# Four projection tiles instead of three in the first k-loop, other warm-up products, and another order on VectorE around the first norm

## The chip, the cores and the metric

The kernel runs on one core of a Trainium2 chip. The metric is the device time of one execution in microseconds; less is better. Before the change three runs gave 1147.17, 1147.83 and 1149.77 us, median 1147.83 us.

## The reference

One transformer block in float32 on 1024 tokens of width 1024. Only its beginning matters here:

```python
mod = jax.nn.silu(c) @ w_ada[l] + b_ada[l]
sh1, sc1, g1, sh2, sc2, g2 = jnp.split(mod, N_MOD, axis=-1)
h = rms_norm(x, norm1_g[l]) * (1.0 + sc1[:, None]) + sh1[:, None]
z = h @ w_in[l]                     # 1024 x 1024 times 1024 x 2048
q = z[..., :A]; k = z[..., A:2*A]; v = z[..., 2*A:3*A]; u = z[..., 3*A:]
```

q, k and v go on to differential attention (q and k with a partial rotary), u to a pooling mixer; an output projection, a second norm, a routed mixture of 32 experts and a final norm follow.

## The kernel before

The kernel holds everything transposed: `xt[k]` is the k-th of eight blocks of 128 channels by 1024 tokens. Float32 products are made from halves: a value is split into a high part (ScalarE copies it to a shorter float, names in `h`) and a low part (VectorE subtracts the high part, names in `l`), and a product of two values is three matmuls, high by high, low by high, high by low. `split` (line 113) does this for every weight tile.

The stage of this case is the first projection, z = h w_in. Its 2048 output columns are 16 tiles of 128, in the order of `ORDER` (line 39): qr, kr, v0, q0, k0, u3, v1, u2 and so on. Tile m has its weights in `win`, split by `w_split(m)` into `wih` and `wil`; its sum stands in PSUM (`pz_...`), as 2 halves x 8 blocks k x 3 matmuls = 48 matmuls of 128x512.

Ahead of it (lines 308 to 339) the squares of `xt` are summed on ScalarE and VectorE (`ssq`), reduced on TensorE (`pss`), raised to the power -1/2 on GpSimd (`xr`), spread over all partitions by TensorE (`prs`, PSUM), and copied to SBUF by ScalarE (`rstd`). `warm` (line 317) issues matmuls whose result nobody reads, `pwarm`: 4 on each of four `xt` blocks as they land (`WARM`) and 8 between `pss` and `prs` (`WARM1`), each 128x128.

Then for each block k (lines 729 to 752): `norm1` multiplies `xt[k]` by `rstd` on VectorE, `norm1_high` makes `hh[k]` on ScalarE with the scale and shift of the conditioning (`gs`, `sh`), `norm1_rest` writes the unsplit value over `xt[k]` on ScalarE, `norm1_low` subtracts on VectorE (`hl[k]`). The scale and shift of block k are two sums over a 128x1024 slab of w_ada (`wa_sum`, VectorE, names in `wt`), finished by two small ScalarE instructions (`wa_add`). The loop runs two norms ahead and multiplies tiles 0 to 2 by block k as soon as that block is there; tile 0 and 1 are open in one PSUM pool (`pt`), tile 2 in another (`pw`). After the loop the code walks all 16 tiles: for m > 2 it multiplies tile m with all eight blocks at once, splits the weights of tile m + 1, evicts the finished tile, and lets VectorE do one or more of 32 further slab sums (`mod_row`, `MODS`).

The order on each engine is the order of the code: every instruction of TensorE, VectorE, ScalarE and GpSimd is kept in program order, and SyncE issues its DMAs in order. A tile framework adds the semaphore waits.

Of the kernel before, what the change touches and what calls it, by code (L numbers as in the profile page):

```python
# [13 lines left out]
AF = mybir.ActivationFunctionType  # L14
OP = mybir.AluOpType
# [3 lines left out]
P = 128  # L19
D = 1024  # L20
S = 1024
T = S // P
KD = D // P
# [15 lines left out]
ORDER = ["qr", "kr", "v0", "q0", "k0", "u3", "v1", "u2", "q1", "k1", "u1", "q2", "k2", "u0", "v2", "v3"]  # L39
# [13 lines left out]
STACK = (9, 10, 14)  # L53
FIRST = (16 - START) // 2
ML = 6
WARM = {3: 4, 4: 4, 5: 4, 6: 4}
WARM1 = 8
DOWN = 4
WQ = 5
YN = 2  # L60
# [7 lines left out]
def block_kernel(ctx: ExitStack, tc: tile.TileContext, A):  # L68
# [20 lines left out]
    def slab(name, shape=(1024,), dt=F32):  # L89
        n = int(np.prod(shape))  # L90
        t = big.tile([P, 1024], dt, name=name, tag="s")[:, :n]
        if len(shape) == 2:
            t = t.rearrange("p (a b) -> p a b", a=shape[0])
        elif len(shape) == 3:
            t = t.rearrange("p (a b c) -> p a b c", a=shape[0], b=shape[1])
        return t
# [4 lines left out]
    def dma(dst, src):  # L101
        tc.keep_in_program_order(nc.sync.dma_start(dst, src))  # L102
# [7 lines left out]
    def f(ap):  # L110
        return ap.bitcast(F32)

    def split(src, hi, lo, eng=None):
        act.activation(hi, src, AF.Copy)
        if eng is pool:
            pool_tt(lo, src, f(hi), OP.subtract)
        else:
            dve.tensor_tensor(lo, src, f(hi), op=OP.subtract)
# [31 lines left out]
    xt = []  # L150
# [93 lines left out]
    with tc.tile_pool(name="ps0", bufs=2, space=PSUM) as psum, tc.tile_pool(name="ps1", bufs=2, space=PSUM) as psum1, \  # L244
# [6 lines left out]
        def pt(name, shape=(1024,)):  # L251
            return shaped(psum.tile([P, 1024], F32, name=name, tag="p"), shape)

        def pw(name, shape):
            return shaped(psum1.tile([P, 512], F32, name=name, tag="w"), shape)
# [14 lines left out]
        def w_load(m):  # L270
            w = slab(f"win{m}", (KD, P))
            dma(w, A["w_in"][m])
            wsp[m] = w

        def w_split(m, eng=None):
            w = wsp[m]
            hi, lo = slab(f"wih{m}", (KD, P), F32R), slab(f"wil{m}", (KD, P), F32R)
            split(w, hi, lo, eng)
            wsp[m] = hi, lo
# [12 lines left out]
        def wa_sum(k, i):  # L292
            w = WA.pop((k, i))
            dve.scalar_tensor_tensor(w, w, 1.0, cB, op0=OP.mult, op1=OP.mult, accum_out=(gs, sh)[i][:, k:k + 1])

        def wa_add(k):
            for c, b, g in ((gs, bsc, n1g[:, k:k + 1]), (sh, bsh, 1.0)):
                c = c[:, k:k + 1]
                act.activation(c, c, AF.Identity, bias=b[:, k:k + 1], scale=g)
# [5 lines left out]
        w_load(1)  # L305
        wa_load(2)
        w_load(2)
        ssq = slab("ssq")
        for k in range(KD):
            sq = slab(f"sq{k}") if k else ssq  # L310
# [6 lines left out]
        def warm(x, n):  # L317

            for _ in range(n):
                pe.matmul(pwarm[:, 0:P], ident, x[:, 0:P], start=True, stop=True)  # L320

        for k, n in WARM.items():
            warm(xt[k], n)
# [7 lines left out]
        warm(xt[0], WARM1)  # L331
        prs = rows(pt("prs"), r8)
        rstd = slab("rstd")
        wa_sum(1, 0)
        w_split(0)
        wa_add(0)
        wa_sum(1, 1)
        act.activation(rstd, prs, AF.Copy)
        wa_add(1)

        hh, hl = [], []

        def norm1(k):
            dve.tensor_tensor(xt[k], xt[k], rstd, op=OP.mult)

        def norm1_high(k):
            hh.append(slab(f"hh{k}", dt=F32R))
# [17 lines left out]
        def project(m, h, ks, parts=(0, 1)):  # L365
            hi, lo = wsp[m]
            if m not in PZ:
                p = pt("pz_" + ORDER[m]) if m != 2 else None
                PZ[m] = [pw(f"pz_{ORDER[m]}_{i}", (512,)) if p is None else p[:, i * 512:(i + 1) * 512] for i in range(2)]
                PF[m] = p  # L370
            cs = slice(h * 512, (h + 1) * 512)
            for k in ks:
                if 0 in parts:
                    pe.matmul(PZ[m][h], hi[:, k], hh[k][:, cs], start=(k == 0), stop=False)
                    pe.matmul(PZ[m][h], lo[:, k], hh[k][:, cs], start=False, stop=False)
                if 1 in parts:
                    pe.matmul(PZ[m][h], hi[:, k], hl[k][:, cs], start=False, stop=(k == KD - 1))
# [58 lines left out]
        def plain(nm, pz):  # L436

            hi, lo = slab("th" + nm, dt=F32R), slab("tl" + nm, dt=F32R)
            if nm[0] == "q":
                act.activation(hi, pz, AF.Copy, scale=0.125)  # L440
                dve.scalar_tensor_tensor(lo, pz, 0.125, f(hi), op0=OP.mult, op1=OP.subtract)
            else:
                split(pz, hi, lo)
            yield
            qk_store(nm, hi, lo)

# [266 lines left out]
            wa_load(k)  # L713
        dma(rope_c, A["rope"][0])
        dma(rope_s, A["rope"][1])
        w_load(3)
        w_load(4)
        dma(wpe, A["w_pool"])
        dma(wr, A["w_r"])
        for n in range(ML):  # L720
# [2 lines left out]
        def project3(k, ms):  # L723
            for lo in range(2):
                for m in ms:
                    for h in range(2):
                        project(m, h, (k,), (lo,))

        for k in (0, 1):
            norm1(k)  # L730
        w_split(1)
        for k in range(KD):
            if k > 1:
                wa_add(k)
            norm1_high(k)
            if k == 1:
                w_split(2)
            norm1_rest(k)
            for n in {0: (2,), 1: (3,), 2: (4, 5), 4: (6, 7)}.get(k, ()):
                wa_sum(n, 0)  # L740
                wa_sum(n, 1)
            norm1_low(k)
            if k + 2 < KD:
                norm1(k + 2)
            if k == 0:
                project3(0, (0, 1))
            elif k == 1:
                project3(0, (2,))
            if k:
                project3(k, (0, 1, 2))  # L750
            if k >= 6:
                w_split(k - 3)
        done = 0
        for m, nm in enumerate(ORDER):
            if m > 2 and m + 2 < 16:
                w_load(m + 2)
            if m > 3 and m + 1 < 16:
                w_split(m + 1)
            if m > 2:
                if m >= START:  # L760
                    n, j = divmod(m - START, 2)
                    score(n, j)
                    row_max(n, j)
                    expo(n, j)
                    if n and j == 0:
                        combine(n - 1)
                project(m, 0, range(KD))
                if m == 15:
                    run_later()
                project(m, 1, range(KD))  # L770
            pz = PZ.pop(m)
            pz = PF[m] if m != 2 else pz
            if nm[0] in "uv":
                g = {"u": pool_mix, "v": values}[nm[0]](int(nm[1]), pz)
            else:
                g = (rope if nm[1] == "r" else plain)(nm, pz)
            next(g, None)
            if m == 15:
                combine(FIRST - 1)
            if m > 2:  # L780
                run_later()
            later.append(g)
            if m == 3:
                lamt = slab("lamt", (4, 64))
                bcast_row(lamt.rearrange("p a b -> p (a b)"), A["lam"], 256)
                lam2 = slab("lam2", (2, 64))
                lams = cst.tile([P, 4], F32, name="lams")
                nlam = lams[:, 3:4]
                subg8 = cst.tile([P, 1], F32, name="subg8")
                dve.tensor_tensor(lam2, lamt[:, 0:4:2], lamt[:, 1:4:2], op=OP.mult)  # L790
                dve.tensor_reduce(lams[:, 0:2], lam2, axis=AX.X, op=OP.add)
                act.activation(lams[:, 0:2], lams[:, 0:2], AF.Exp)
                dve.tensor_sub(lams[:, 2:3], lams[:, 0:1], lams[:, 1:2])
                dve.tensor_scalar(nlam, lams[:, 2:3], LAM0, -1.0, op0=OP.add, op1=OP.mult)
                dve.tensor_scalar(nlam, nlam, LAM_MAX, -LAM_MAX, op0=OP.min, op1=OP.max)
                dve.tensor_scalar(subg8, subg, 1.0 - LAM0, None, op0=OP.mult)
            for _ in range(MODS.get(m, 0)):
                mod_row(done)
                mod_load(done + ML)
                done += 1  # L800
            if m in ROWS:
                later.append(row_out(ROWS.index(m)))
                next(later[-1], None)
            if WO <= m < WO + 8:
                later.append(wo_part(m - WO))
                next(later[-1])
            if m == ROWS[2] + 2:
                later.append(router_weights())
                next(later[-1])
            for part in range(3):  # L810
                if m == STACK[part]:
                    stack_load(0, part)
# [631 lines left out]
```

## Time and profile before

| | us |
|---|---|
| median of three runs | 1147.83 |
| the profiled execution | 1144.32 |
| its span, first to last instruction | 1142.3 |
| TensorE busy | 1091.3 |
| VectorE busy | 971.2 |
| first product of the projection | at 29.38 |
| product stream of tile 6 (v1) begins | at 108.26 |

All times on engines are from the profiled execution, counted from its first instruction. PE is TensorE, PEld its weight load, DVE VectorE, ACT ScalarE, POOL GpSimd, SP SyncE. In a timeline row the bracket at the end gives the idle time of that engine just before, and what ended it. The granted clock of TensorE is given as a share of 2.4 GHz: 0.50 is 1.2 GHz. Nearly all operations are recorded by one helper (line 81), so rows are told apart by the tile's name.

### The profile page before, as it was taken

The numbers are of one execution on the slowest core, as the hardware profiler recorded it, in microseconds if no ns is written. First come the engines' busy times: TensorE is split into PE (matmuls) and PEld (weight loads), VectorE is DVE, ScalarE is ACT, GpSimd is POOL, SyncE is SP. The second block draws the span as 40 slices with busy tenths as digits, with TensorE's granted clock in tenths as the row PEclk, the third lists the DMA queues.
The fourth block names the chain that finished last, engine by engine and source line by source line (L and its number), as shares of the span: only waits on it lengthen the run. The fifth ranks groups of instructions, "written<-read, shape, count | busy, mean of one in ns | idle before, by whom it ended". The sixth has DMA issues, their size and how long they took to land.

```text
span 1142.3 us, 15812 instructions
## 1 busy us (share of the span) xinstructions
PE 1091.3 (96%) x5351; PEld 895.7 (78%) x5351; DVE 971.2 (85%) x1235; ACT 726.7 (64%) x932; POOL 245.7 (22%) x195
## 2 busy tenths in 40 slices
PE   6898998999999999989999999999999999999984
PEld 6687876778888778878888888888888888888852
DVE  5977787689999675887999999999999999999957
ACT  5651133378888102216888888888888888888812
POOL 1000000168888102211231011010110111101032
PEclk8899999999999999978999999999999999999998
DMA  9949599797735724548999999999999999999673
GB/s 366 380 159 346 212 327 332 312 237 206 203 95 194 284 111 167 205 162 307 405 389 383 375 387 389 381 394 379 384 390 377 389 379 384 385 380 383 257 302 147
DMA packets 103863, 349.61 MB, mean 306 GB/s; under 512 B 16771, under 2 KB 17699, under 8 KB 103779
## 3 DMA queue, kind: packets, MB, share of 16 engines
q1 hardware_dynamic: 92034, 322.82, 76.7%
q0 software_dynamic: 11456, 24.96, 5.7%
q8 instruction: 43, 0.70, 0.3%
q10 hardware_dynamic: 288, 0.79, 0.2%
q14 instruction: 42, 0.34, 0.1%
HBM read 309.95 MB, written 55.33 MB: 320 GB/s over the span
## 4 chain that ended last, share of the span: by engine, by line
PE 49%; DVE 2%; DMA 2%; issue 0%; ACT 0%; POOL 0%; SPq 0%; DVEq 0%; ACTq 0%
PE pg L81 30%; PE py L81 15%; PE px L81 3%; DMA fy<-yd 2%; DVE fy L81 2%; PE pht L81 1%; DVE wl L81 0%; ACT wh L81 0%; SPq L102 0%; POOL frs L81 0%; ACT fy L81 0%; POOL fy L81 0%; DVEq L1440 0%; DVE hx L81 0%; ACT y L81 0%
## 5 line engine op out<-in xcount | busy, mean ns | idle before, releaser
L81 DVE TENSOR_TENSOR wl<-we,wh 128x1024 fp32r<-128x1024 f32 x384 | 458.7, 1222 | 40.9 <-ACT wh L81 32.5
L81 ACT ACTIVATE wh<-we 128x1024 fp32r<-128x1024 f32 x384 | 399.9, 1058 | 58.3 <-PE pg L81 26.1
L81 PE MATMUL pg<-wh,xs 128*128 128x512 f32 x1024 | 338.7, 397 | 0.0
L81 PEld LDWEIGHTS pg<-wh,xs 128*128 128x128 f32 x1024 | 192.9, 188 | 39.4 <-DVE xs L81 0.6
L81 PE MATMUL pg<-wl,xs 128*128 128x512 f32 x512 | 200.3, 391 | 0.0
L81 PE MATMUL py<-wh,hth 128*128 128x512 f32 x512 | 172.3, 398 | 0.7 <-ACT hth L81 0.7
L81 POOL DMA_INDIRECT yd<-y,ix x31 | 30.7, 992 | 427.3 <-ACT y L81 426.7
L81 PEld LDWEIGHTS py<-wh,hth 128*128 128x128 f32 x512 | 96.9, 189 | 21.0 <-ACT hth L81 0.9
L81 PEld LDWEIGHTS pg<-wl,xs 128*128 128x128 f32 x512 | 96.7, 189 | 18.3
L81 PE MATMUL py<-wl,hth 128*128 128x512 f32 x256 | 100.5, 393 | 0.0
L81 ACT ACTIVATE e<-s,mx 128x1024 f32<-128x1024 f32 x64 | 71.7, 1120 | 28.9 <-DVE mx L81 25.9
L81 DVE TENSOR_REDUCE mx<-s 128x1 f32<-128x1024 f32 x64 | 78.2, 1222 | 5.9 <-PE s L81 3.2
L81 PE MATMUL s<-k,sq 128*128 128x512 f32 x256 | 72.5, 405 | 5.4 <-ACT e L81 5.3
L81 POOL TENSOR_TENSOR e<-e,e 128x1024 f32<-128x1024 f32 x32 | 76.5, 2391 | 2.7
L81 POOL DMA_INDIRECT x<-xnd,ix x32 | 48.2, 1505 | 64.7 <-PE px L81 43.7
L81 PE MATMUL po<-wh,v 128*128 128x256 f32 x256 | 60.8, 302 | 0.0
L81 DVE SCALAR_TENSOR_TENSOR wt<-wt,cB 128x1024 f32<-128x1024 f32 x48 | 56.3, 1220 | 0.8 <-ACT cB L81 0.8
L81 POOL TENSOR_SCALAR e<-e,cc 128x1024 f32<-128x1024 f32 x32 | 39.2, 1225 | 81.7 <-DVE cc L81 70.6
L81 PEld LDWEIGHTS py<-wl,hth 128*128 128x128 f32 x256 | 48.5, 189 | 9.5
L81 PEld LDWEIGHTS s<-k,sq 128*128 128x128 f32 x256 | 44.1, 189 | 14.1 <-ACT e L81 7.5
L81 DVE SCALAR_TENSOR_TENSOR x<-pm,Y,x 128x1024 f32<-128x1024 f32 (+1 forms) x33 | 41.3, 1251 | 15.9 <-PE pm L81 14.8
L81 ACT ACTIVATE xn<-x 128x1024 f32<-128x1024 f32 x7 | 7.4, 1062 | 69.2 <-DVE x L81 51.2
(247 smaller groups left out, 1853.6 us busy)
## 6 DMA issues: line engine op xcount, KB each, us to landing
we<-in_w_exp SPq DMA_DIRECT2D x384, 512.0 KB
wt<-in_w_ada SPq DMA_DIRECT2D x48, 512.0 KB
win<-in_w_in SPq DMA_DIRECT2D x16, 512.0 KB
woB<-wod SPq DMA_DIRECT2D x16, 512.0 KB
fy<-yd SPq DMA_DIRECT2D x16, 512.0 KB
k<-kd SPq DMA_DIRECT2D x32, 192.0 KB
xt<-in_xT SPq DMA_DIRECT2D x8, 512.0 KB
wo<-in_w_out SPq DMA_DIRECT2D x8, 512.0 KB
```

The costliest lines, as they stand in the source:

```text
L81: ins = getattr(self.eng, op)(*args, **kw)
```

## The change

Four things. The k-loop now multiplies four tiles by each block instead of three (`DEEP`); q0, the fourth, is summed in the third PSUM pool (`po`) and evicted in halves. The loads and splits of weights move one tile ahead with it: `w_load(3)` goes in front of the slab loads for k = 3 and later, tile 3 is split at k = 1, tiles 4 and 5 at k = 6 and 7. The products that nobody reads are 128x512 instead of 128x128, in other numbers (2, 2, 1, 1, 1, 1, 1 on `xt[1]` to `xt[7]`, one after `pss`), and two new ones read `xt[0]` after its norm (`WARM2`). And the order around the first norm changes: `norm1(0)` reads `prs` in PSUM instead of its copy, the slab sums of block 1 and the split of tile 1 come after it, the loop runs one norm ahead instead of two, and each block does exactly the sums of the next.

```diff
-WARM = {3: 4, 4: 4, 5: 4, 6: 4}
-WARM1 = 8
+WARM = {1: 2, 2: 2, 3: 1, 4: 1, 5: 1, 6: 1, 7: 1}
+WARM1 = 1
+WARM2 = 2
+DEEP = 4
...
         w_load(2)
+        w_load(3)
...
-                pe.matmul(pwarm[:, 0:P], ident, x[:, 0:P], start=True, stop=True)
+                pe.matmul(pwarm, ident, x[:, 0:512], start=True, stop=True)
...
         rstd = slab("rstd")
-        wa_sum(1, 0)
         w_split(0)
         wa_add(0)
-        wa_sum(1, 1)
         act.activation(rstd, prs, AF.Copy)
-        wa_add(1)
...
         def norm1(k):
-            dve.tensor_tensor(xt[k], xt[k], rstd, op=OP.mult)
+            dve.tensor_tensor(xt[k], xt[k], rstd if k else prs, op=OP.mult)
...
-        w_load(3)
         w_load(4)
+        w_load(5)
...
-        for k in (0, 1):
-            norm1(k)
-        w_split(1)
+        norm1(0)
+        warm(xt[0], WARM2)
         for k in range(KD):
-            if k > 1:
+            if k:
                 wa_add(k)
             norm1_high(k)
             if k == 1:
                 w_split(2)
             norm1_rest(k)
-            for n in {0: (2,), 1: (3,), 2: (4, 5), 4: (6, 7)}.get(k, ()):
-                wa_sum(n, 0)
-                wa_sum(n, 1)
+            if k == 0:
+                w_split(1)
+            if k + 1 < KD:
+                wa_sum(k + 1, 0)
+                wa_sum(k + 1, 1)
+                norm1(k + 1)
             norm1_low(k)
-            if k + 2 < KD:
-                norm1(k + 2)
+            if k == 1:
+                w_split(3)
             if k == 0:
                 project3(0, (0, 1))
             elif k == 1:
-                project3(0, (2,))
+                project3(0, (2, 3))
             if k:
-                project3(k, (0, 1, 2))
+                project3(k, range(DEEP))
             if k >= 6:
-                w_split(k - 3)
+                w_split(k - 2)
         done = 0
         for m, nm in enumerate(ORDER):
-            if m > 2 and m + 2 < 16:
+            if m > 3 and m + 2 < 16:
                 w_load(m + 2)
-            if m > 3 and m + 1 < 16:
+            if m > 4 and m + 1 < 16:
                 w_split(m + 1)
-            if m > 2:
+            if m > 3:
...
                 project(m, 1, range(KD))
```

The order on VectorE from the low part of tile 0's weights on, with the semaphores that each instruction waits for. `wil` is the low part of a weight tile, `wt` a slab of w_ada, `xt_72` and `xt_74` blocks 0 and 1, `hl` the low part of a block. Before:

```order
L81 TENSOR_TENSOR wil_240<-win_150,wih_239 128x1024 [waits DMAHW4_49,Activation_49]
L81 SCALAR_TENSOR_TENSOR wt_1_154,sh<-wt_1_154,cB 128x1024 [waits DMAHW6_49]
L81 TENSOR_TENSOR xt_72<-xt_72,rstd 128x1024 [waits Activation_49]
L81 TENSOR_TENSOR xt_74<-xt_74,rstd 128x1024
L81 TENSOR_TENSOR wil_297<-win_156,wih_296 128x1024 [waits DMAHW7_49,Activation_49]
L81 SCALAR_TENSOR_TENSOR wt_2_158,gs<-wt_2_158,cB 128x1024 [waits DMAHW0_49]
L81 SCALAR_TENSOR_TENSOR wt_2_160,sh<-wt_2_160,cB 128x1024 [waits DMAHW1_49]
L81 TENSOR_TENSOR hl_305<-xt_72,hh_300 128x1024 [waits Activation_49]
L81 TENSOR_TENSOR xt_76<-xt_76,rstd 128x1024
L81 TENSOR_TENSOR wil_325<-win_162,wih_324 128x1024 [waits DMAHW2_49,DVE_49,Activation_49]
```

With the change, from the same place to the low part of tile 3's weights:

```order
L83 TENSOR_TENSOR xt_72<-xt_72,prs 128x1024 [waits Activation_49]
L83 TENSOR_TENSOR wil_285<-win_156,wih_284 128x1024 [waits DMAHW7_49,Activation_49]
L83 SCALAR_TENSOR_TENSOR wt_1_152,gs<-wt_1_152,cB 128x1024 [waits DMAHW5_49]
L83 SCALAR_TENSOR_TENSOR wt_1_154,sh<-wt_1_154,cB 128x1024 [waits DMAHW6_49]
L83 TENSOR_TENSOR xt_74<-xt_74,rstd 128x1024
L83 TENSOR_TENSOR hl_291<-xt_72,hh_281 128x1024
L83 TENSOR_TENSOR wil_312<-win_162,wih_311 128x1024 [waits DMAHW2_49,DVE_49,Activation_49]
L83 SCALAR_TENSOR_TENSOR wt_2_158,gs<-wt_2_158,cB 128x1024 [waits DMAHW0_49]
L83 SCALAR_TENSOR_TENSOR wt_2_160,sh<-wt_2_160,cB 128x1024 [waits DMAHW1_49]
L83 TENSOR_TENSOR xt_76<-xt_76,rstd 128x1024
L83 TENSOR_TENSOR hl_319<-xt_74,hh_309 128x1024 [waits DVE_49,Activation_49]
L83 TENSOR_TENSOR wil_322<-win_164,wih_321 128x1024 [waits DMAHW3_49,DVE_49,Activation_49]
```

The norm of block 0 still waits for ScalarE although it now reads `prs`, and the low part of tile 3's weights stands eleven instructions behind it.

The order on ScalarE from the copy `rstd` on. Before, the high part of tile 1's weights (`wih_296`) stood ahead of block 0:

```order
L81 ACTIVATE rstd<-prs 128x1024 [waits PE_49]
L81 ACTIVATE gs<-gs,cols 128x1 [waits DVE_49]
L81 ACTIVATE sh<-sh,cols 128x1 [waits DVE_49]
L81 ACTIVATE wih_296<-win_156 128x1024 [waits DMAHW7_49,Activation_49]
L81 ACTIVATE hh_300<-xt_72,sh,gs 128x1024 [waits DVE_49]
L81 ACTIVATE xt_72<-xt_72,sh,gs 128x1024 [waits Activation_49]
```

With the change:

```order
L83 ACTIVATE rstd<-prs 128x1024 [waits PE_49]
L83 ACTIVATE hh_281<-xt_72,sh,gs 128x1024 [waits DVE_49]
L83 ACTIVATE xt_72<-xt_72,sh,gs 128x1024 [waits PE_49,Activation_49]
L83 ACTIVATE wih_284<-win_156 128x1024 [waits DMAHW7_49]
L83 ACTIVATE gs<-gs,cols 128x1 [waits DVE_49]
L83 ACTIVATE sh<-sh,cols 128x1 [waits DVE_49]
L83 ACTIVATE hh_309<-xt_74,sh,gs 128x1024 [waits DVE_49,Activation_49]
L83 ACTIVATE wih_311<-win_162 128x1024 [waits DMAHW2_49]
L83 ACTIVATE xt_74<-xt_74,sh,gs 128x1024 [waits Activation_49]
L83 ACTIVATE wih_321<-win_164 128x1024 [waits DMAHW3_49]
```

The high part of tile 1's weights now stands behind both instructions on block 0, and the second of these waits for TensorE, whose two new products read the same `xt_72`.

The order on TensorE at the end of block 0. Before, tile v0 followed the low parts of qr and kr, and then came block 1 (`hh_322`):

```order
L81 MATMUL pz_kr<-hl_305,wih_296 128x512 x2
L81 MATMUL pz_v_0_334<-hh_300,wih_324 128x512
L81 MATMUL pz_v_0_334<-hh_300,wil_325 128x512
L81 MATMUL pz_v_1_335<-hh_300,wih_324 128x512
L81 MATMUL pz_v_1_335<-hh_300,wil_325 128x512
L81 MATMUL pz_v_0_334<-hl_305,wih_324 128x512
L81 MATMUL pz_v_1_335<-hl_305,wih_324 128x512
L81 MATMUL pz_qr<-hh_322,wih_239 128x512
```

With the change tile q0 stands between v0 and block 1:

```order
L83 MATMUL pz_qr<-hl_291,wih_226 128x512 x2
L83 MATMUL pz_kr<-hl_291,wih_284 128x512 x2
L83 MATMUL pz_v_0_325<-hh_281,wih_311 128x512
L83 MATMUL pz_v_0_325<-hh_281,wil_312 128x512
L83 MATMUL pz_v_1_326<-hh_281,wih_311 128x512
L83 MATMUL pz_v_1_326<-hh_281,wil_312 128x512
L83 MATMUL pz_q_0_331<-hh_281,wih_321 128x512
L83 MATMUL pz_q_0_331<-hh_281,wil_322 128x512
```

All products of block 1 and later stand behind the last of these rows, which needs the low part of tile 3's weights.

## Rows read from the trace of the kernel before

**Rows 1.** The page: busy time, share and instructions of each engine; chain by engine.
```profile
PE 1091.3 (96%) x5351; PEld 895.7 (78%) x5351; DVE 971.2 (85%) x1235; ACT 726.7 (64%) x932; POOL 245.7 (22%) x195
PE 49%; DVE 2%; DMA 2%; issue 0%; ACT 0%; POOL 0%; SPq 0%; DVEq 0%; ACTq 0%
```

**Rows 2.** Waits of TensorE: what waited for what, us in all, times, longest.
```profile
PE pz_u L81 <- DVE wil L81: 3.1, 1, 3.1
PE pz_qr L81 <- DVE hl L81: 2.1, 3, 0.8
```

**Rows 3.** Timeline, all engines, 19 to 30 us: start, us, engine, operation.
```profile
19.02 3.76 PE L81 MATMUL pwarm<-xt,ident 128*128 128x128 f32 x16
19.45 2.55 POOL L81 TENSOR_TENSOR xr<-xr_m,mhalf 128x8 f32<-128x8 f32 x1 [17.63 <-DVE xr_m L81]
22.57 3.16 PE L81 MATMUL prs<-ident,xr 128*128 128x128 f32 x16
25.77 1.02 ACT L81 ACTIVATE rstd<-prs 128x1024 f32<-128x1024 f32 x1 [4.94 <-PE prs L81]
26.83 2.36 DVE L81 TENSOR_TENSOR xt<-xt,rstd 128x1024 f32<-128x1024 f32 x2 [2.90 <-ACT rstd L81]
27.15 1.04 ACT L81 ACTIVATE wih<-win 128x1024 fp32r<-128x1024 f32 x1
28.10 1.23 ACT L81 ACTIVATE hh<-xt,sh,gs 128x1024 fp32r<-128x1024 f32 x1
29.10 1.22 DVE L81 TENSOR_TENSOR wil<-win,wih 128x1024 fp32r<-128x1024 f32 x1
29.36 1.24 ACT L81 ACTIVATE xt<-xt,sh,gs 128x1024 f32<-128x1024 f32 x1
29.38 0.79 PE L81 MATMUL pz_qr<-hh,wih 128*128 128x512 f32 x1 [3.65 <-ACT hh L81]
```

**Rows 4.** Windows of TensorE: stretch, length, busy (records), granted clock, DMA, GB/s.
```profile
22.00:25.00 3.00, 3.00 (x16) 0.50 1.03 412
25.00:28.00 3.00, 0.73 (x6) 0.98 1.02 404
29.00:38.00 9.00, 7.97 (x18) 0.50 1.03 410
39.00:96.00 57.00, 52.31 (x231) 1.00 0.68 249
97.00:100.00 3.00, 3.00 (x9) 0.50 1.01 306
```

**Rows 5.** Timelines of ScalarE, TensorE and VectorE from 68 to 146 us.
```profile
68.53 1.03 ACT L81 ACTIVATE zqr<-pz_qr 128x1024 f32<-128x1024 f32 x1 [4.42 <-PE pz_qr L81]
...
80.65 1.03 PE L81 MATMUL pv<-ident,vt 128*128 128x128 f32 x8
81.44 0.48 PE L81 MATMUL pz_k<-hh,wih 128*128 128x512 f32 x1
...
95.86 0.50 PE L81 MATMUL pz_u<-hh,wil 128*128 128x512 f32 x1 [3.06 <-DVE wil L81]
...
100.30 1.22 DVE L81 TENSOR_TENSOR wil<-win,wih 128x1024 fp32r<-128x1024 f32 x1
...
108.26 0.39 PE L81 MATMUL pz_v<-hh,wih 128*128 128x512 f32 x1
...
109.59 0.25 DVE L81 COPY ends<-ub 128x16 f32<-128x16 f32 x2 [8.07 <-ACT ub L81]
...
118.25 1.22 DVE L81 TENSOR_TENSOR wil<-win,wih 128x1024 fp32r<-128x1024 f32 x1
...
119.18 0.47 PE L81 MATMUL pz_u<-hh,wih 128*128 128x512 f32 x1
...
142.10 1.88 PE L81 MATMUL py<-us,wpe 128*128 128x512 f32 x4
...
144.49 1.40 DVE L81 SCALAR_TENSOR_TENSOR mul<-py,cols,muh 128x512 fp32r<-128x512 f32 x2
```

More of the change, by code (lines that the diff above doesn't have):

```diff
@@ L367, in project @@
             if m not in PZ:
-                p = pt("pz_" + ORDER[m]) if m != 2 else None
-                PZ[m] = [pw(f"pz_{ORDER[m]}_{i}", (512,)) if p is None else p[:, i * 512:(i + 1) * 512] for i in range(2)]
+                p = pt("pz_" + ORDER[m]) if m not in (2, 3) else None
+                PZ[m] = [(pw, po)[m - 2](f"pz_{ORDER[m]}_{i}", (512,)) if p is None else p[:, i * 512:(i + 1) * 512]
+                         for i in range(2)]
                 PF[m] = p
@@ L438, in plain @@
             hi, lo = slab("th" + nm, dt=F32R), slab("tl" + nm, dt=F32R)
[L439 to L443, printed above, removed]
+            for p, cs in zip(pz, (slice(0, 512), slice(512, S))) if isinstance(pz, list) else ((pz, slice(0, S)),):
+                if nm[0] == "q":
+                    act.activation(hi[:, cs], p, AF.Copy, scale=0.125)
+                    dve.scalar_tensor_tensor(lo[:, cs], p, 0.125, f(hi[:, cs]), op0=OP.mult, op1=OP.subtract)
+                else:
+                    split(p, hi[:, cs], lo[:, cs])
             yield
@@ L771, in block_kernel @@
             pz = PZ.pop(m)
-            pz = PF[m] if m != 2 else pz
+            pz = PF[m] if m not in (2, 3) else pz
             if nm[0] in "uv":
```

## The prediction, made before the change was run

> **What bounds the kernel now.** I read the page first: TensorE is busy 96% of the span, and of the engines the chain that ended last names almost only TensorE [rows 1]. So time is won or lost where TensorE stands still or runs slowly, and a delay there moves everything behind it. The list of waits comes next: of those of the first 120 us the change touches 3.1 us for a weight split ahead of tile u3 and 2.1 us for low parts of blocks in the k-loop [rows 2]. The windows with the granted clock follow: half speed (0.50) from 22 to 25, almost full from 25 to 28 after that busy stretch, half again from 29 to 38 after the idle time ahead of the first product, full from 39 to 96, half from 97 to 100 after the wait ahead of u3 [rows 4]. Last come the timelines of the two places where the order moves [rows 3, 5].
>
> Three prices from rows. Tile v1 runs without a wait: 48 products from 108.26 to 119.18, 0.2275 us each. Tile u3, after its wait, took 12.40 us for 47 products (95.86 to 108.26), where 47 x 0.2275 would be 10.69: a restart at half clock costs 1.7 us [rows 5]. VectorE does two norms in 2.36 us, one operation in 1.22, so 1.14 for each further one [rows 3].
>
> **The change part by part.** *The first norm.* The copy `rstd` starts at 25.77 and takes 1.02, the norm follows at 26.83 [rows 3]. The new norm reads PSUM, but in the built order its only wait is for ScalarE, and the one ScalarE instruction that reads `prs` is that copy: the norm still comes after it. I cost this edit at nothing; were the two to run side by side it would be 1.05 us earlier, and that is its lower end. The Trainium skill (PSUM — Partial Sum Buffer, "PSUM bank collisions raise a hardware error") says that reads of one bank by ScalarE and VectorE must not overlap and are ordered by a dependency. By it the sum is as here, without it 1.05 us less; the trace of before, where VectorE reads the copy, doesn't show it.
>
> *Warm-up products ahead of it.* `prs` starts at 22.57 though GpSimd is done at 22.00: the eight narrow products run until 22.78 [rows 3]. One wide product in their place ends earlier, so `prs` can start some 0.4 us sooner, but then runs wholly at half clock. I take 0.2 us; the ends are 0 and 0.5. First norm: 26.6 to 27.85.
>
> *The two products on block 0.* No row shows one at this place. Two float32 products of 128x512 take 1.88 us at full clock [rows 5], so 3.76 at half. In the trace the clock falls shortly after 28 [rows 4]; with 0.6 us at full and the rest at half they end at 31.05; the ends are 29.8 and 31.6. They hide nothing: `norm1_rest(0)` writes the same block, waits for them, and stands ahead of the high part of tile 1's weights on ScalarE. That gives 31.05 + 1.24 + 1.04 = 33.35 for the high part, and the low part of tile 1 starts there on VectorE, where it started at 29.10 before [rows 3]. Before, `wih` of tile 1 was done at 28.19, while the norm ran.
>
> *VectorE from there to tile 3's weights.* In order: tile 1 low (33.35), two sums, norm 1 (at 33.35 + 3 x 1.14 = 36.8, done 38.0), `hl[0]` (done 39.1). Tile 2 low needs `hh[1]` and then `wih` of tile 2 on ScalarE: 38.0 + 1.23 + 1.04 = 40.3. Then five at 1.14: two sums, norm 2, `hl[1]`, and tile 3 low at 46.0, done at 47.25. TensorE takes its products in order, so the second product of q0 waits until 47.3, and all of block 1 behind it. By then 17 of the 4 x 48 = 192 products are done.
>
> *The loop.* 175 products x 0.2275 = 39.8, plus one restart at half clock, since TensorE has mostly waited from 33 to 47: 1.7. The loop ends at 88.8. Before, the same products (tiles 0 to 3) were done at 80.65, when `pv` starts [rows 5]: 8.15 later. In the loop itself the waits of 2.1 us [rows 2] vanish, since a block now gives TensorE 24 x 0.2275 = 5.5 us against four operations of 1.14 on VectorE; this is contained in the 175.
>
> *After the loop.* `pv` transposes what ScalarE has evicted. Before, tile 3 covered that eviction; now `zqr` starts about 1.2 us ahead of the loop's end, at 87.6 (six products follow the last of qr), `zkr` and the two halves of v0 follow, and `pv` ends at about 91.1 instead of 81.44: +9.7. Tiles k0 and u3 then run without a wait, since tile 5 was split inside the loop: 91.1 + 2 x 10.9 = 112.9, against 108.26: +4.65. Here the 3.1 us of wait and the 1.7 us of restart are won back.
>
> *The split of tile 6.* From `zqr` (68.53) to the low part of tile 6 (100.30) VectorE works almost without a gap for 31.8 us [rows 5]: ropes, slab sums, low parts, two weight splits. One of the two splits has moved into the loop, 1.14 less; the low part of q0 in halves adds about 0.18, as another operation in two halves takes 1.40 against 1.22. So 30.8 us: from 87.6 to 118.4, done at 119.6. Before, TensorE had three tiles to multiply meanwhile; now it has two, is done at 112.9, does one product of v1 and waits for 6.5 us. Its second product was at 108.5 and comes at 119.65: +11.15. The wait is twice that ahead of u3, so I charge a restart again, 1.7: +12.85. Then it ends: tile 7's low part comes 8.66 us after VectorE turns to u3 (109.59 to 118.25), so by 129.5, and u2 starts at 119.18 + 12.85 = 132.0.
>
> The Trainium skill (TensorE: Matmul & The Clock Gate, "HAM oscillation — how this bites in real kernels") says that gaps in which TensorE idles bring the throttled clock back each time. The trace agrees at 29 and 97 [rows 4]. By it both restarts are paid; if wide products kept the clock at full, both would be saved, the third rival below.
>
> *The sum.* 8.15 + 1.55 (`pv`) - 5.05 (u3) + 6.5 (wait) + 1.7 = +12.85. The profiled execution goes from 1144.32 to 1157.2; it stands 3.5 us under the median of the runs, so on the median 1147.83 + 12.9 = 1160.7. Lower end: the two products at full clock (-1.25) and no restart (-3.4) give +8.2, 1156.0. Upper end: those products at half clock (+0.55), each restart twice as dear, as the first stretch at half clock was much longer than the second [rows 4], (+3.4): +16.8, 1164.6. Slab DMAs for k = 3 and later move back by one load of 512 KB, over 10 us ahead of their sums: nothing.
>
> **Rivals.** *The late wait does not come.* If VectorE had tile 6 split by 112.9, the sum would stop at +4.65: 1152.5. For it speaks that VectorE has idle time near the loop's end; against it, that every operation of those 31 us waits for an evicted tile of the loop or stands behind one that does.
>
> *TensorE is never short of data (the other side).* Were tile 3's low part there when TensorE has done its 17 products, about 37, the loop would run through from 29.8: 43.7 plus 1.7 of half clock, end at 75.2, `zqr` at 74.0, tile 6 split at 106.0, 2.5 us ahead of before: 1145.3, with a restart 1147.0. It decides for this case if that low part ends by 37. Against it: eleven operations behind the norm are 12.5 us even without any wait for ScalarE, so 40.4 at best.
>
> *The wide products keep the clock at full.* Then the lower end holds: 1156.0. For it: the clock rose at 25 after a busy stretch [rows 4]. Against it: between `prs` and the loop TensorE now waits as long as before, and later twice.
>
> *The first norm does start beside the copy.* 1.05 less, 1159.7; the rest stays.
>
> **How the numbers follow.** The forecast, with its own range from 1158 to 1165, gets 0.65, the first norm's rival included; the clock kept 0.2; no late wait 0.07; the other side 0.05; 0.03 for what I do not see. 0.2% of the time, 2.3 us, is what a measurement can tell from no change. Faster by more (under 1145.5) gets part of the other side: 0.03. Within it: 0.04. Slower: 0.93. The range from 1153 to 1165 leaves out the other side and part of the case without the late wait.
>
> **What the profile will show.** The first norm starts at 26 to 27, after the copy ends. The high part of tile 1's weights ends behind 32 instead of at 28.2. TensorE waits for VectorE at the second product of q0, ending at 45 to 48, and again, 4 to 7 us, at the second product of v1. In the loop after block 1 it waits for nothing. The wait ahead of u3 is gone. `pv` waits 1 to 2 us for ScalarE. The prediction is wrong if the second product of q0 comes before 42, if v1 does not wait, or if some later stage takes back the delay, so that the distance from v1 to the end is shorter than before.

## The result, and the profile after

The changed kernel takes 1161.26 us (median of 4 runs, 1159.25 to 1163.76) where the kernel before takes 1147.5: ratio 1.0122, 95% interval 1.0101 to 1.0143. Run again later beside other kernels it took 1159.47 against 1146.80: 1.0109 (1.0088 to 1.0131). It is slower by 12.7 to 13.8 us, as forecast (1160.7). The profiled execution took 1159.25, 14.9 more than that of before.

The page, as in [rows 1] (busy time):

```profile
PE 1097.3 (95%) x5327; PEld 893.2 (77%) x5327; DVE 970.7 (84%) x1236; ACT 728.1 (63%) x933; POOL 245.2 (21%) x195
```

Nothing here tells of a loss: TensorE is busy 6 us longer and 95% of the span. The waits of TensorE in the first 130 us, against [rows 2], do:

```profile
PE pz_v L83 <- DVE wil L83: 4.0, 1, 4.0
PE pz_q L83 <- DVE wil L83: 4.0, 1, 4.0
PE pz_qr L83 <- DVE hl L83: 3.6, 1, 3.6
...
PE pz_v L83 <- DVE tlk L83: 2.0, 1, 2.0
```

The wait of 3.1 us ahead of u3 is gone, and so are those inside the loop. In their place stand a wait for block 0's low part (3.6), one for tile 3's low weights (q0, 4.0), and two at v1: 2.0 for the low part of k0 (`tlk`) and 4.0 for tile 6's low weights. The timeline from 21 to 49 us, which answers [rows 3], shows how the first two come about:

```profile
21.89 3.78 PE L83 MATMUL prs<-ident,xr 128*128 128x128 f32 x16 [1.74 <-POOL xr L83]
...
25.70 1.02 ACT L83 ACTIVATE rstd<-prs 128x1024 f32<-128x1024 f32 x1 [5.04 <-PE prs L83]
26.76 1.22 DVE L83 TENSOR_TENSOR xt<-xt,prs 128x1024 f32<-128x1024 f32 x1 [5.29 <-ACT rstd L83]
...
28.04 3.78 PE L83 MATMUL pwarm<-xt,ident 128*128 128x512 f32 x4 [2.37 <-DVE xt L83]
...
31.93 1.24 ACT L83 ACTIVATE xt<-xt,sh,gs 128x1024 f32<-128x1024 f32 x1 [2.67 <-PE pwarm L83]
...
33.07 1.04 ACT L83 ACTIVATE wih<-win 128x1024 fp32r<-128x1024 f32 x1
...
34.14 1.23 DVE L83 TENSOR_TENSOR wil<-win,wih 128x1024 fp32r<-128x1024 f32 x1 [6.16 <-ACT wih L83]
...
39.98 1.22 PE L83 MATMUL pz_qr<-hl,wih 128*128 128x512 f32 x2 [3.57 <-DVE hl L83]
...
46.82 1.22 DVE L83 TENSOR_TENSOR wil<-win,wih 128x1024 fp32r<-128x1024 f32 x1
...
48.09 0.79 PE L83 MATMUL pz_q<-hh,wil 128*128 128x512 f32 x1 [3.99 <-DVE wil L83]
```

Read it from the bottom up: q0's second product (48.09) needs tile 3's low part (46.82), the last of a queue on VectorE that starts with tile 1's low part (34.14); that one waited for ScalarE's high part (33.07), which stands behind the rest of block 0 (31.93), and that waited 2.67 us for the two wide products. VectorE had nothing to do for 5.29 us ahead of the norm and for 6.16 behind it. The granted clock, against [rows 4] (columns: stretch, length, busy time and instructions of PE, PEld, DVE, ACT and POOL, clock, DMA share, GB/s):

```profile
20.00:28.00 8.00, 3.93 (x17) 3.49 (x16) 2.70 (x4) 1.32 (x2) 1.92 (x2) 0.50 1.03 410
28.00:33.00 5.00, 4.96 (x8) 2.52 (x8) 0.00 (x0) 2.31 (x2) 0.00 (x0) 0.50 1.03 411
34.00:36.00 2.00, 1.08 (x3) 0.68 (x4) 1.86 (x2) 0.11 (x1) 0.00 (x0) 1.00 1.02 406
37.00:43.00 6.00, 3.02 (x7) 2.02 (x8) 4.82 (x6) 4.41 (x5) 0.00 (x0) 0.50 1.03 410
44.00:47.00 3.00, 0.10 (x1) 0.00 (x0) 3.00 (x5) 1.44 (x2) 0.00 (x0) 0.99 1.06 398
48.00:53.00 5.00, 4.91 (x12) 3.85 (x13) 5.00 (x8) 2.46 (x5) 0.00 (x0) 0.50 0.99 394
...
119.00:125.00 6.00, 3.69 (x9) 2.92 (x10) 6.00 (x11) 0.00 (x0) 0.00 (x0) 0.50 1.00 345
...
211.00:214.00 3.00, 3.00 (x8) 2.34 (x8) 1.89 (x2) 1.01 (x2) 0.00 (x0) 0.50 1.03 411
```

The clock is at half from 20 to 33, and the two wide products run at half. It is at full from 34 to 36, behind the busy stretch from 28 to 33, and at half again from 37, in and behind the wait of 3.6 us that ends at 39.98. During most of q0's wait (44 to 47) it is at full; the products behind that wait, and those behind v1's, run at half. Last, the place behind the loop, against [rows 5]:

```profile
91.86 1.15 PE L83 MATMUL pv<-ident,vt 128*128 128x128 f32 x8 [1.16 <-ACT vt L83]
...
116.83 0.47 PE L83 MATMUL pz_v<-hh,wih 128*128 128x512 f32 x1 [2.05 <-DVE tlk L83]
...
120.03 1.22 DVE L83 TENSOR_TENSOR wil<-win,wih 128x1024 fp32r<-128x1024 f32 x1
...
121.31 0.79 PE L83 MATMUL pz_v<-hh,wil 128*128 128x512 f32 x1 [4.00 <-DVE wil L83]
...
134.08 0.48 PE L83 MATMUL pz_u<-hh,wih 128*128 128x512 f32 x1
...
223.01 1.88 PE L83 MATMUL py<-us,wpe 128*128 128x512 f32 x4
```

Tile u2 starts at 134.08 where it started at 119.18: 14.9 later, about what the end shows. Behind it a little is taken and given back. In the kernel before the last of these rows is:

```profile
206.16 1.88 PE L81 MATMUL py<-us,wpe 128*128 128x512 f32 x4
```

So the distance is 16.9 us at 223, behind the stretch at half clock from 211 to 214, which the kernel before does not have; at the end, by the spans (1157.5 and 1142.3), it is 15.2.

### The profile page after: what moved, and what is told of

Read it like the earlier page. It is cut to its first block, busy times and chain, and to the rows that moved or that the text cites. A ratio compares the mean times of both kernels' runs of the same rounds, so it can differ in the third digit from the quotient of the medians.

```text
span 1157.5 us, 15771 instructions
## 1 busy us (share of the span) xinstructions
PE 1097.3 (95%) x5327; PEld 893.2 (77%) x5327; DVE 970.7 (84%) x1236; ACT 728.1 (63%) x933; POOL 245.2 (21%) x195
## 4 chain that ended last, share of the span: by engine, by line
PE 48%; DVE 2%; DMA 2%; issue 0%; ACT 0%; POOL 0%; SPq 0%; DVEq 0%; ACTq 0%; POOLq 0%
PE pg L83 30%; PE py L83 15%; PE px L83 3%; DVE fy L83 2%; DMA fy<-yd 2%; PE pht L83 1%; DVE wl L83 0%; ACT wh L83 0%; POOL frs L83 0%; POOL fy L83 0%; ACT fy L83 0%; SPq L104 0%; DVEq L1444 0%; DVE hx L83 0%; ACT y L83 0%
```

## The experiments

Each was timed beside the kernel before; times are medians, and each ratio is to the kernel before as timed beside that experiment. Two runs of one kernel differ by up to 0.9%, so the traces carry the single microseconds and the times the sum.

**1. Without the two wide products on block 0.**
```diff
-WARM2 = 2
+WARM2 = 0
```


> The kernel after without the two wide products on block 0 that follow the first norm. Theory (they hold ScalarE's rest of block 0, and with it tile 1's weights): the rest of block 0 starts at 29.2 instead of 31.93 us, tile 1's low part on VectorE at about 31.4 instead of 34.14, the second product of q0 at 45.4 instead of 48.1, and since all behind it is a chain, the whole is 2.7 us shorter: 1158.6 against 1161.3. Rival (the two products buy TensorE's clock something): a longer stretch at half clock in the loop, and the time the same or up to 3 us longer, 1161 to 1164.

1155.54, ratio 1.0078 (1.0055 to 1.0101). The timeline:
```profile
31.57 1.23 DVE L83 TENSOR_TENSOR wil<-win,wih 128x1024 fp32r<-128x1024 f32 x1 [3.53 <-DMA wt<-in_w_ada]
...
45.52 0.79 PE L83 MATMUL pz_q<-hh,wil 128*128 128x512 f32 x1 [3.62 <-DVE wil L83]
```
```profile
34.00:36.00 2.00, 0.50 (x2) 0.00 (x0) 2.00 (x3) 0.66 (x2) 0.00 (x0) 0.50 1.02 408
```
Tile 1's low part and q0's second product come 2.57 us earlier than in the kernel after, close to the 2.7 expected; in time it is 0.3 to 0.45% less than the two measurements of the kernel after, and 2.7 us (0.23%) lie within what the intervals allow. (The bracket of the first row names a DMA; ScalarE's high part of tile 1 ended at 31.54, just ahead of it.) The products cost the 2.67 us for which they hold ScalarE. They did change the clock: from 34 to 36 it is at half without them and at full with them. No time came of that, since TensorE waits for weights there.

**2. Tile 1's weights split first, the two products kept.**
```diff
         norm1(0)
+        w_split(1)
         warm(xt[0], WARM2)
...
-            if k == 0:
-                w_split(1)
```


> The kernel after with the split of tile 1's weights issued right behind the first norm, ahead of ScalarE's work on block 0, and the two wide products kept. Theory: tile 1's low part runs at 28 instead of 34.1 us, the two sums and the second norm behind it move up, tile 3's low part ends at about 42.7 instead of 48.0, the loop ends 5.2 us earlier, the late wait at v1 stays at 4 us: 1156. Rival (the loop's end is set by TensorE's products at half clock, not by when data come): under 1 us gained.

1153.37, ratio 1.0068 (1.0044 to 1.0092), 0.4 to 0.55% under the kernel after (1156 expected).
```profile
42.90 0.80 PE L83 MATMUL pz_q<-hh,wil 128*128 128x512 f32 x1 [4.38 <-DVE wil L83]
```
q0's second product moves from 48.09 to 42.90, 5.2 us, although in this execution the first norm ran 1.05 us later. The loop's end is set by when tile 3's low weights come.

**3. The first norm reads the copy again.**
```diff
-            dve.tensor_tensor(xt[k], xt[k], rstd if k else prs, op=OP.mult)
+            dve.tensor_tensor(xt[k], xt[k], rstd, op=OP.mult)
```


> The kernel after with the first norm reading the copy rstd in SBUF again. Theory: the norm starts at 26.8 us in both, since it waited for ScalarE either way, and the time is the same, 1161.3 within 1. Rival (the direct read saves the copy's time or the norm runs faster or slower from PSUM): norm 1.0 us later and 1162.3.

1162.68, ratio 1.0144 (1.0115 to 1.0172), no different from the kernel after.
```profile
25.82 1.02 ACT L83 ACTIVATE rstd<-prs 128x1024 f32<-128x1024 f32 x1 [4.90 <-PE prs L83]
...
26.87 1.23 DVE L83 TENSOR_TENSOR xt<-xt,rstd 128x1024 f32<-128x1024 f32 x1 [5.15 <-ACT rstd L83]
```
The norm starts 0.03 us behind the end of the copy (25.82 + 1.02), and in the kernel after 0.04 behind it (25.70 + 1.02, then 26.76): reading `prs` itself saves nothing, as the norm waits for the copy either way. The time alone could not tell this from the rival's 1162.3; the trace does.

**4. Six modulation sums moved to the loop's end.**
```diff
-MODS = {0: 1, 1: 2, 2: 2, **{m: 3 for m in range(3, 12)}}
+TAIL = 6
+MODS = {3: 2, **{m: 3 for m in range(4, 12)}}
...
         done = 0
+        for _ in range(TAIL):
+            mod_row(done)
+            mod_load(done + ML)
+            done += 1
         for m, nm in enumerate(ORDER):
```


> The kernel after with six of the modulation sums that VectorE does behind tiles 0 to 3 issued at the end of the k-loop, where VectorE idles for 15.7 us. Theory (the wait at v1 is VectorE's work between the first rope and tile 6's split, no longer covered by a third tile): 6 x 1.145 = 6.9 us leave that stretch, tile 6's low part runs at 113.1 instead of 120.0, the waits of 2.05 and 4.0 us at v1 vanish with the restart of 2.0 us: 8.1 shorter, 1153.2. Rival (the wait at v1 has another cause, the load or ScalarE's split): v1 waits as before and the time stays at 1161.

1151.88, ratio 1.0038 (1.0018 to 1.0058): 0.7 to 0.85% under the kernel after, expected 0.7%.
```profile
112.54 1.22 DVE L84 TENSOR_TENSOR wil<-win,wih 128x1024 fp32r<-128x1024 f32 x1
...
114.21 0.39 PE L84 MATMUL pz_v<-hh,wil 128*128 128x512 f32 x1
...
124.90 0.47 PE L84 MATMUL pz_u<-hh,wih 128*128 128x512 f32 x1
```
Tile 6's low part comes 7.5 us earlier, v1 does not wait, and its 48 products take 10.9 us without a restart. u2 starts 9.2 us ahead of the kernel after, 0.6 of them because the loop ended earlier in this execution (`pv` at 91.22 for 91.86). So the late wait is VectorE's work between the loop and tile 6's split.

**5. The kernel before with the wide warm-up products.**
```diff
-WARM = {3: 4, 4: 4, 5: 4, 6: 4}
-WARM1 = 8
+WARM = {1: 2, 2: 2, 3: 1, 4: 1, 5: 1, 6: 1, 7: 1}
+WARM1 = 1
...
-                pe.matmul(pwarm[:, 0:P], ident, x[:, 0:P], start=True, stop=True)
+                pe.matmul(pwarm, ident, x[:, 0:512], start=True, stop=True)
```


> The kernel before with nothing changed but the warm-up products ahead of the norms: the wide ones of the kernel after (ten on blocks 1 to 7 and one ahead of prs) in place of the narrow ones; no product after the norm. Theory (the idle time of TensorE between prs and the k-loop sets the clock of the loop, whatever ran before it): the granted clock rises about 8 us earlier than 14.9, but is at half from about 20 and again at the loop's start, and the time is 1147.5 within 1.5. Rival (wide products keep the clock up): the stretch at half clock at the loop's start, 10.2 us before, vanishes or halves, and 2.5 to 5 us are gained: 1142.5 to 1145.

1145.27 against 1144.82, ratio 0.9998 (0.9981 to 1.0015): nothing. Windows and one line of the timeline:
```profile
29.00:33.00 4.00, 3.78 (x8) 2.51 (x8) 4.00 (x6) 4.00 (x4) 0.00 (x0) 0.50 1.03 410
34.00:46.00 12.00, 9.11 (x40) 6.87 (x38) 12.00 (x18) 6.01 (x8) 0.00 (x0) 1.00 1.03 405
47.00:50.00 3.00, 3.00 (x8) 2.34 (x7) 3.00 (x4) 2.79 (x4) 0.00 (x0) 0.50 1.04 414
```
```profile
46.00 0.73 PE L81 MATMUL pz_qr<-hl,wih 128*128 128x512 f32 x2 [2.06 <-DVE hl L81]
```
The clock is at half at the loop's start here too. The half-clock stretch at the loop's start was shorter than in [rows 4], and still no time was won: VectorE is busy for all 12 us from 34 to 46, so the faster TensorE waits 2.06 us for it at 46.00, and behind that wait the clock is at half once more (47 to 50). Which of the two, VectorE's pace or the second stretch at half, ate the gain is not separated.

**6. The kernel before with the fourth tile, and no other part of the change.**
```diff
+DEEP = 4
...
+            if k == 1:
+                w_split(3)
...
-                project3(0, (2,))
+                project3(0, (2, 3))
             if k:
-                project3(k, (0, 1, 2))
+                project3(k, range(DEEP))
             if k >= 6:
-                w_split(k - 3)
+                w_split(k - 2)
```


> The kernel before with the fourth tile in the k-loop and what it needs (its load and split, its PSUM, the order of loads and splits behind it), and nothing else: narrow warm-up products, the sums and norms in the order of before, the norm from the copy. Theory (four tiles need a third weight split on VectorE before block 1 can be multiplied, and take away the tile that covered VectorE's work behind the loop): tile 3's low part ends at about 41.9 us, so q0's second product waits 4 us for it; 175 products of 0.2275 and a restart of 2.6 end the loop at 84.3 instead of 90.5; v1 waits 2 + 4 us as in the kernel after: 1161.3 - 6.2 = 1155. Rival (the fourth tile is what could have helped, and only the new order of sums and norms costs): 1147 or less.

1154.37, ratio 1.0072 (1.0048 to 1.0097). Waits of TensorE from 26 to 130 us:
```profile
PE pz_v L82 <- DVE wil L82: 4.0, 1, 4.0
PE pz_q L82 <- DVE wil L82: 4.0, 1, 4.0
```
The waits at q0 (ending at 41.97) and at v1 are there without the new order. So of the loss of 1.1 to 1.2%, 0.7% comes with the fourth tile as the old order feeds it, and 0.4 to 0.5% from the new order of sums, split and wide products. The traces say the same: u2 starts at 128.03 here, 8.85 us behind the kernel before and 6.05 us ahead of the kernel after.

**7. Four tiles, with data in time.** The old warm-up products and the norm from the copy; the rest so:
```diff
+        wa_sum(1, 0)
+        w_split(1)
+        wa_sum(1, 1)
         act.activation(rstd, prs, AF.Copy)
+        wa_add(1)
...
+        for k in (0, 1):
+            norm1(k)
         for k in range(KD):
...
+            if k == 0:
+                norm1_rest(0)
+                norm1_low(0)
+            if k == 1:
+                w_split(2)
+                w_split(3)
+            if k:
+                norm1_rest(k)
+                if k + 1 < KD:
+                    wa_sum(k + 1, 0)
+                    wa_sum(k + 1, 1)
+                    norm1(k + 1)
+                norm1_low(k)
```
and the six sums at the loop's end, as in 4.

> Four tiles in the k-loop, narrow warm-up products, the sums of block 1 and the split of tile 1's weights in the time in which VectorE and ScalarE wait for prs, two norms first, the splits of tiles 2 and 3 ahead of the sums of block 2, and six modulation sums at the loop's end. Theory (each place where TensorE waited is supplied in time): the products of block 0 start at 29.6 us as before and no product of the loop waits, half clock until about 39 as before, loop end at 77.5; no wait at v1; u2 starts near 113, 6 us ahead of the kernel before: 1141.5. Rival (TensorE's clock falls in spite of it, or VectorE is late further on, at u2 or q1): 1146 to 1150.

1135.98 against 1144.82, ratio 0.9901 (0.9874 to 0.9928). All waits of TensorE from 26 to 130 us, and a window:
```profile
PE pz_qr L83 <- ACT hh L83: 3.7, 1, 3.7
PE pv L83 <- ACT vt L83: 1.2, 1, 1.2
```
```profile
33.00:74.00 41.00, 40.57 (x179) 33.06 (x177) 38.98 (x54) 22.32 (x29) 0.00 (x0) 1.00 0.75 286
```
u2 starts at 108.41, 4.6 us ahead of the expectation, and the time is 5.5 us under it, of which 2.7 are the kernel before's own, timed beside it (1144.82 for 1147.5). The loop began at 27.86 and not at 29.6; that need not be the edit's, since experiment 9, which has the code of before up to the loop's end, began it at 27.83. And the expectation had taken over from [rows 4] a stretch of 9 us and more at half clock, which here was over before 33.

**8. The same, with TensorE kept busy ahead of the loop** by wide products on `cB`, which no later step writes; the warm-up products on the `xt` blocks are wide here too, as in the kernel after, with one more on block 7:
```diff
+WARM1 = 4
+WARM2 = 4
...
+        warm(cB, WARM1)
         prs = rows(pt("prs"), r8)
...
+        warm(cB, WARM2)
         for k in (0, 1):
             norm1(k)
```


> The same with wide warm-up products, and with TensorE kept busy where it waited: four wide products on the conditioning block cB (which nothing writes later) between the sum of squares and prs, and four between prs and the loop. Theory (idle time ahead of the loop is what brings half clock): the granted clock stays at full from about 6 us to behind the loop, four wide products take 3.76 each time, the loop starts at 29.1 and ends near 74.5, u2 starts 2.7 us earlier than without them: 1138.8. Rival (the clock falls anyway): prs is held by wide products at half clock (1.87 each) and starts 2.5 us later, the loop 3 to 6 us later and runs at half clock: 1145 to 1150.

1136.43, ratio 0.9910 (0.9886 to 0.9934): no gain over 7, although the clock did what the theory said: u2, expected 2.7 us earlier than in 7, starts at 108.37. Windows, and one line of ScalarE:
```profile
15.00:28.00 13.00, 12.11 (x52) 6.92 (x51) 11.16 (x15) 8.20 (x12) 2.64 (x2) 1.00 1.03 409
28.00:33.00 5.00, 3.96 (x16) 2.58 (x16) 3.08 (x3) 5.00 (x5) 0.00 (x0) 1.00 1.03 408
...
185.00:188.00 3.00, 2.90 (x7) 1.80 (x7) 2.46 (x4) 0.61 (x2) 0.00 (x0) 0.50 1.00 399
```
```profile
179.86 1.06 ACT L84 ACTIVATE wih<-win 128x1024 fp32r<-128x1024 f32 x1 [6.18 <-DMA win<-in_w_in]
```
At full clock the products of block 0 wait 1.05 us in two places for VectorE (0.40 at 30.34, 0.65 at 32.42), which 7 does not do at half clock; the loop ends at the same time in both (`pv` at 74.68 and 74.73). In this execution the load of tile 13 came late besides, and with it a wait of 3.3 us at 184.6; the clock fell to half behind it.

**9. The kernel before with four sums at the loop's end**, the edit of 4 with `TAIL = 4` and `MODS = {2: 1, ...}`.

> The kernel before with four of the modulation sums that VectorE does behind tiles 0 to 2 issued at the end of its k-loop, where VectorE idles for 4.7 us; nothing else. Theory (the wait ahead of u3 is the same VectorE stretch that made v1 wait in the kernel after): 4 x 1.145 = 4.6 us leave that stretch, the wait of 3.1 us ahead of u3 and its restart of 1.7 vanish: 4.8 less, 1142.5 where before has 1147.3. Rival (VectorE is late elsewhere, or the first rope is pushed back): within 1 us of before.

1140.40 against 1146.80, ratio 0.9951 (0.9929 to 0.9974). Nothing waits for tile 5's weights any more; of over 0.2 us the list of waits from 26 to 130 us has, beside the one ahead of the first product, but the loop's own:
```profile
PE pz_qr L82 <- DVE hl L82: 3.8, 3, 1.7
```
The gain is 6.4 us where 4.8 was expected. So about half of what 7 wins needs neither a fourth tile nor a new order of the norms.

**10. Version 7 with three tiles** (and four sums at the loop's end, since its loop ends sooner).

> The combination of the four-tile kernel with early splits (narrow warm-up products), but with three tiles in the k-loop, and four sums in place of six at its end. Theory (with data in time the fourth tile gives TensorE 5.5 us of work for each block against VectorE's four operations, 4.6 us, and three tiles only 4.1): TensorE waits about 0.5 us in each block, u3 waits 1.0 us for its split, v1 starts 3.6 us later than with four tiles: 1139.6 where the four-tile kernel has 1136.0. Rival A (the number of tiles makes no difference once the order is right): 1136 to 1137. Rival B (nearly all of the gain is the fourth tile's): 1143 or more.

1139.64 against 1146.80, ratio 0.9935 (0.9915 to 0.9956). v1 starts at 101.03 where version 7 has 97.50, 3.5 us as expected, 0.4 of them because the loop began at 28.29 and not at 27.86. The intervals of 7 and 10 just overlap, so the time alone does not settle the fourth tile's share; the traces agree with it.

**11. Version 8 with the loads of tiles 6 to 15 one tile earlier.**
```diff
-                w_load(m + 2)
+                w_load(m + 3)
...
         w_load(5)
+        w_load(6)
```


> The combination with TensorE kept busy ahead of the loop, with the loads of tiles 6 to 15 issued one tile earlier. Theory (what the full clock gained at the loop was lost again near 184 us, where ScalarE's split of tile 13 waited until 179.86 for its load and held the exponentials behind it, a wait of 3.3 us on TensorE and a restart): that wait vanishes, 2.5 to 4 us less than 1136.4, so 1133. Rival (that wait comes from the order of ScalarE's own work or belongs to that one execution): 1136.4 within 1.

1133.46 against 1146.80, ratio 0.9887 (0.9866 to 0.9908), the lowest of all, though its interval overlaps those of 7 and 8. Tile 13 is split 7.6 us earlier, without a wait, and from the warm-up products to 400 us no window shows the clock under full; one of them:
```profile
172.30 1.04 ACT L84 ACTIVATE wih<-win 128x1024 fp32r<-128x1024 f32 x1
```
```profile
185.00:400.00 215.00, 206.75 (x1233) 174.85 (x1232) 179.19 (x298) 133.79 (x242) 122.40 (x68) 1.00 0.66 205
```
The late load does not come from the change. The kernel before has the same wait on ScalarE:
```profile
188.18 1.06 ACT L81 ACTIVATE wih<-win 128x1024 fp32r<-128x1024 f32 x1 [5.08 <-DMA win<-in_w_in]
```
Whether version 7, or the kernel before, with the loads earlier would gain as much was not tried.

**12. The kernel after once more.**

> The kernel after, unchanged, once more beside the others. Theory: 1.2 to 1.4% over before, 1161 where before has 1147; the waits at q0 and v1 as in its first profile. Rival (part of its 13.8 us was that chip's): under 1% over before.

1159.47, ratio 1.0109 (1.0088 to 1.0131), a little under the 1.2 to 1.4% expected, with waits of 3.7 us at q0 and of 2.0 and 4.0 at v1.
```profile
48.12 0.80 PE L83 MATMUL pz_q<-hh,wil 128*128 128x512 f32 x1 [3.69 <-DVE wil L83]
...
90.59 1.15 PE L83 MATMUL pv<-ident,vt 128*128 128x128 f32 x8 [1.16 <-ACT vt L83]
...
120.03 0.80 PE L83 MATMUL pz_v<-hh,wil 128*128 128x512 f32 x1 [4.01 <-DVE wil L83]
...
133.73 0.48 PE L83 MATMUL pz_u<-hh,wih 128*128 128x512 f32 x1
```
The waits are those of the first profile within 0.3 us, and the prices of the restarts are not: from q0's second product to `pv` it is 42.5 us here and 43.8 there, so that restart cost 1.3 us and not 2.6; from v1's second product to u2 it is 13.7 us and 12.8, so that one cost 3.0 and not 2.1.

## Why the prediction was right, step by step

The result, the sign and the chain came out. On the profiled execution the sum was 2.05 us short (12.85 for 14.9): 0.8 for the two products, 0.9 for the first restart, 0.4 for the second. On the medians it was not (13.8 and 12.7). That the forecast hit the first median to 0.6 us is in part luck: the profiled execution of before, from which the sum starts, lay 3.2 us under its median, that of the changed kernel 2.0 us.

- *First norm at nothing:* right. It started at 26.76, for 26.6, and experiment 3 shows that the edit is worth nothing. The Trainium skill (PSUM — Partial Sum Buffer, "PSUM bank collisions raise a hardware error") says that the compiler's scheduler puts a dependency between ScalarE's and VectorE's reads of one bank; the trace agrees, with 0.04 us from the copy's end to the norm.
- *Two products until 31.05:* they ended at 31.82, since none of them ran at full clock. With their 0.77 us tile 1's low part (34.14 for 33.35) and q0's second product (48.09 for 47.3) were late by as much; 48.09 lies just outside the 45 to 48 of the prediction. Experiments 1 and 2 confirm the chain.
- *Loop end at 88.8:* it ended at about 90.5. The restart was mis-sized: 175 products at 0.2275 are 39.8 us and took 42.4, so it cost 2.6 and not 1.7. The 1.7 came from u3, one execution of one wait. The length of the wait does not set the price: in experiment 12 the same kernel paid 1.3 here after almost the same waits.
- *`pv` 9.7 later, u3 done at 112.9, tile 6's low part at 119.6:* 11.2 later, 114.8, 121.25. The terms held; each carries the 1.7 us from above. That v1's first product also waits, for the low part of k0 (2.05), was not foreseen; it cost nothing, as its second product had to wait until 121.31 in any case.
- *Second restart 1.7:* 2.1 (47 products from 121.31 to 134.08), and 3.0 in experiment 12.
- *The rivals.* The late wait came (rival one wrong). Against that rival the prediction had said that every operation ahead of tile 6's split waits for an evicted tile or stands behind one that does; experiment 4 shows that six of them only stood behind, by the order of the code, and removes the wait by moving them. TensorE was short of data (rival two wrong). That the wide products keep the clock at full was wrong for where they stand: the windows from 20 to 33 show 0.50. With more of them, on data that nobody waits for, the clock was at full there (experiment 8). That the rival failed on the gaps of 1.7 and 2.4 us that were left on both sides of `prs` is likely but not shown, as the number of the products differs too.
- *On clock and gaps:* the Trainium skill (TensorE: Matmul & The Clock Gate, "HAM oscillation — how this bites in real kernels") has it that idle gaps bring the slow clock back. The traces agree: the waits of 3.1 us ahead of u3 before, of 4.0 at q0 and at v1 after, and of 3.3 in version 8 are each followed by products at 0.50, and version 11, without such waits, has no window at 0.50 up to 400 us. Shorter waits were followed by it too: 2.06 us in experiment 5, and in the kernel after, from 211, none over 1.5 us.

## What to carry to other kernels

A deeper accumulation loop takes away the tile that covered another engine's work behind the loop, and needs one more operand before its first pass can end: count both before the depth. Work that only fills a slow engine (here VectorE's modulation sums) belongs in the stretches where that engine waits; here the same six sums cost 8 to 9 us in the chain and nothing in the gap. And products that only keep the clock up should read data that no later step overwrites: on block 0 they held ScalarE for 2.67 us, on `cB` they did not delay the loop (and won no time either).

## What was not expected of the hardware

- The price of a restart is not one number, and the wait does not set it: 1.7 us at u3 before, 2.6 and 2.1 in the first profile of the kernel after, 1.3 and 3.0 in the second (experiment 12), with the same waits. In the first profile it is half of what is left of the stretch at half clock when products flow again: at v1 the windows show 0.50 from 119 to 125, the products flow from 121.31, and 2.1 lost are 4.2 at half.
- Full clock at the loop's start (experiment 8) was worth nothing next to the short stretch at half (experiment 7), as operands came 1.05 us too late for it.
- ScalarE waits for the load of tile 13's weights in every kernel here that was read for it and that issues the loads in the old order: 5.1 us before (until 188.18), 5.5 after (until 203.48), 5.7 in version 7 (until 177.99), 6.2 in version 8 (until 179.86). Of these four only version 8 shows a wait of 3.3 us on TensorE behind it.
